# A hybrid state-space layer: C loaded as four 128-row blocks, B by 64-byte pieces, two reorderings and a PSUM bank of its own

## The chip, the cores and the metric

The kernel runs on one NeuronCore of a Trainium2 chip. The metric is the device time of one execution in microseconds (us); lower is better. Engines are named as in the profile: PE (TensorE), DVE (VectorE), ACT (ScalarE), POOL (GpSimd), SP (SyncE, which issues nearly all DMAs). All arithmetic is on float32 data.

## The reference

One decoder layer on x of 1024 positions x 1024 channels: a norm, an input projection, a state-space mixer (S5) on 512 channels, a gated short convolution on the other 512, an output projection, a residual add and a last norm.

```python
xn = rmsnorm(h, norm_gain[l])
proj = jnp.einsum('bld,dc->blc', xn, w_in[l])
...
bb_re = q_re[..., None] * b_re - q_im[..., None] * b_im
bb_im = q_re[..., None] * b_im + q_im[..., None] * b_re
bu_re = jnp.einsum('blgh,gph->blgp', u32, bb_re)
...
y = (jnp.einsum('blgp,ghp->blgh', s_re, c_re.astype(f32))
     - jnp.einsum('blgp,ghp->blgh', s_im, c_im.astype(f32))
     + d_skip.astype(f32) * u32)
...
h = h + jnp.einsum('blc,cd->bld', y, w_out[l])
return rmsnorm(h, final_norm_gain)
```

There are 32 groups g of 16 channels h, each with 64 complex states p. B is [g, p, h] and C is [g, h, p], each with a real and an imaginary part, 128 KB a part.

## The kernel before

Each matrix is split in a high part and a rest, and a product is the sum of three matmul passes: high x high ("h" in the code's tables), rest of x ("x") and rest of the weight ("l"). x is held as 8 row tiles x0 to x7 (row i of 8 consecutive positions); tiles are worked in four pairs, each of which gives 256 columns of the transposed input, a "quarter".

**The first stage** is an order written out by hand in the string `START`; inside it PE, ACT and DVE keep the order in which the code issues. Its words: `sN` squares row tile N on ACT and accumulates (L192); `nAB` is the norm of two tiles on DVE (L92 to L98 and L203); `tP` transposes pair P on PE (L211); `gP` ("gain") writes that pair's high parts `xh` from PSUM on ACT (L218); `xP` ("rest") writes the rest `xl` on DVE (L224); `uBQ...` are products of column block B with quarter Q on PE (L230), and `U` takes several blocks in turn; `kBH` copies block B's finished half H from PSUM to a tile `us` on ACT (L243) and stores it to HBM with four DMAs (L245); `dN` issues N more steps of the discretisation, a long chain of small DVE operations on [128, 32] tiles (L288); `p0`, `p1`, `p2` transpose parameters on PE (L260 to L265 and L275) and evict them on ACT; `C` copies C into another layout on ACT (L435). Products of four blocks use four PSUM banks (pool `pmm`), so a bank for quarter 2 is free only when `k` has copied that block's first half out. `us` has two buffers, so the third store copy waits for the first one's four stores, and the fourth copy for the second's.

**Parameters.** C and B are loaded with 32 rows (one group each) of 4 KB, C into `craw` (L173, L174), B into the upper 32 rows of `cb` (L176); the word `C` puts C beside it. Then `p1` and `p2` make 32 transposes of [64, 128] on PE (L275), and eight ACT instructions (L277) write b1, b2, c1 and c2 of [128, 32, 16], 128 being 64 states twice, with the signs. The discretisation multiplies b1 and b2 into bb and bs.

**DMAs** are issued by SP in program order and go to one queue on 16 DMA engines. Each DMA holds one of eight semaphores in turn, so SP doesn't issue a DMA before the one issued eight earlier has landed. A copy is cut into pieces, each a run of bytes that is contiguous on both sides.

**The middle stage** works through the string `ORDER`: projections for the convolution (tiles h, c, b, z) on PE, between them the state-space steps. `ssm_prep` makes rr (L499 to L501) and vv (L503 to L505) on DVE, rotation tables ec, and ee. `ssm_lags` multiplies bb and vv on PE (L544, `ps_k`), `ssm_in` and `ssm_out` follow (`ps_s`, `ps_y`). Its weight splits are a copy on ACT (L105) and a subtraction on DVE (L106). They share the four weight buffers with the first stage.

**The last stage** multiplies by w_out by a seven-product scheme on half matrices, for four row pairs j (L819), adds the products to the residual rows xa and xb on DVE (L823), squares them on ACT with accumulation (L826), forms 1/sqrt on DVE (`rsqrt_steps`, L92 to L98) and stores the rows. In the last pair the final product into xb's first half is made in two quarters of 256 columns in the PSUM bank `pw`, each followed by its add, its square, and a multiplication by the gain on POOL (L894). Row xa is scaled on ACT (L886) and stored (L887) before these quarters; xb's halves are scaled on DVE (L898) and ACT (L899) and stored (L901). The bank `pw` also holds the sum of three earlier products, which each quarter accumulates onto.

Of the kernel before, what the change touches and what calls it, by code (L numbers as in the profile page):

```python
# [19 lines left out]
P = 128  # L20
# [5 lines left out]
NB = 4  # L26
# [6 lines left out]
START = ("s0 w0 n0 c s1 W0 n1 W1 w1 t0 L0 g0 L1 U010hl x0 u010x. W2 s2 s3 W3 L2 n23 u20hx u30hx t1 L3 g1 u230l. s4 x1 s5 n45 "  # L33
         "U01231h u01lx. k00 p0 u11lx. k10 t2 u21lx. k20 u31lx. k30 d12 g2 s6 x2 s7 C n67 d12 U01232h u01232l t3 g3 d8 x3 u01232x. "
         "U01233h u03l p1 p2 u03x. k01 u13lx. k11 d u23lx. k21 u33lx. k31")
# [22 lines left out]
def hybrid_kernel(ctx: ExitStack, tc, x, norm_gain, w_in, a_re, a_im, log_dt, b_re, b_im,  # L58
# [70 lines left out]

    cb = big.tile([2 * NG, 3 * S * H], F32, tag="cy", name="cb")  # L130
    cb = cb.rearrange("g (r p h) -> g r p h", h=H, r=3)
    craw = pst.tile([NG, 2, H, S], F32, name="craw")
    lam_r = pst.tile([NG, 2, 2, S], F32, name="lam_r")
# [38 lines left out]
    load((4, 5, 6, 7))  # L172
    nc.sync.dma_start(craw[:, 0], c_re[0])  # L173
    nc.sync.dma_start(craw[:, 1], c_im[0])  # L174
    for k, src in enumerate((b_re, b_im, b_re)):
        nc.sync.dma_start(cb[NG:2 * NG, k], src[0])  # L176

# [73 lines left out]
    c2 = par.tile([P, NG, H], F32, name="c2")  # L251
    b1 = pst.tile([P, NG, H], F32, name="b1")
    b2 = pst.tile([P, NG, H], F32, name="b2")
    dT = par.tile([H, NG], F32, name="dT")

    def transpose_params(part):
# [13 lines left out]
        off = part - 1  # L270
        for q in range(2):
            hs = slice(q * 8, q * 8 + 8)
            ps = psm.tile([P, 8, 2 * NG], F32, tag="sm", name=f"ps_cb{off}{q}")
            for h in range(8):
                PE.transpose(ps[:, h], cb[:, off:off + 2, :, 8 * q + h].rearrange("g r p -> g (r p)"), ident[0:2 * NG, 0:2 * NG])  # L275
            for dst, lo, scale in ((b2 if off else b1, NG, nsgn if off else 1.0), (c2 if off else c1, 0, -1.0 if off else sgn)):
                A.activation(dst[:, :, hs], ps[:, :, lo:lo + NG].rearrange("p h g -> p g h"), AF.Copy, scale=scale)  # L277

# [145 lines left out]
    with tc.manual_schedule(engines={mybir.EngineType.PE, mybir.EngineType.Activation, mybir.EngineType.DVE}):  # L424
        for what in START.split():
# [5 lines left out]
            elif what[0] == "d":  # L431
                discretise(int(what[1:]) if what[1:] else None)
            elif what[0] == "C":
                for k in range(3):
                    A.copy(cb[0:NG, k], craw[:, k % 2].rearrange("g h p -> g p h"))  # L435
            elif what[0] == "c":
# [378 lines left out]
    def mult(ps, op_a, op_b, j, first, cols=slice(0, 512)):  # L815
        out_ = ps[:, 0:cols.stop - cols.start]
        for m, (p, q) in enumerate(((0, 0), (0, 1), (1, 0))):
            for k in range(NB):
                PE.matmul(out_, aq[op_a, j][:, p, k], bq[op_b, k][:, q, cols], start=first and m + k == 0,  # L819
                          stop=m == 2 and k == NB - 1, skip_group_check=True)  # L820

    def add(x, ps):
        V.tensor_tensor(x, x, ps, ADD)  # L823
# [23 lines left out]
    for j in pairs:  # L847
# [36 lines left out]
        for op in ops:  # L884
            op()
        A.activation(xa, ga, AF.Copy, scale=r)  # L886
        nc.sync.dma_start(out_ci[:, 2 * j, :], xa)  # L887
        steps, r = rsqrt_steps([part[:, 2:3], part[:, 3:4], part[:, 4:5]])
        for q in range(2):
            c = slice(q * 256, q * 256 + 256)  # L890
            mult(pw[j][:, c], "A22", "T4", j, False, c)
            add(xb[:, c], pw[j][:, c])
            final_square(xb[:, c], part[:, 3 + q:4 + q])
            Q.tensor_tensor(gb[:, c], xb[:, c], g2b[:, c], MUL)  # L894
            steps.pop(0)()
        for step_ in steps:
            step_()
# [35 lines left out]
```

## Time and profile before

| | us |
|---|---|
| runs | 432.88, 433.24, 431.73 (median 432.88) |
| the profiled execution, its time | 432.44 |
| its span (first to last record) | 430.7 |
| PE busy | 418.2 (97% of the span) |
| DVE busy | 330.1 (77%) |
| ACT busy | 182.5 (42%) |
| POOL busy | 34.6 (8%) |
| mean share of the 16 DMA engines, queue of SP | 35.6% |

A timeline row gives start, length, engine, source line, operation, output <- inputs, shape and count; in brackets stands how long the engine was idle before it and what ended that. Matmuls overlap, so a row's length is a little more than the distance to the next one. A window row gives the window, its length, each engine's busy time (and count) where engines were asked for, the granted TensorE clock as a share of full speed, the mean share of the DMA engines and GB/s. SPq is the sequencer that issues DMAs.

### The profile page before, as it was taken

What the parts mean: (1) busy time and instruction counts of PE and PEld (TensorE: products, weight loads), DVE (VectorE), ACT (ScalarE), POOL (GpSimd) and SP (SyncE); (2) the same over time, 40 slices, a digit from 0 to 9 for tenths busy, and PEclk for the clock granted to TensorE, in tenths of its full rate; (3) what the DMA queues carried; (4) which work ended last, traced back from release to release, by engine and by line L of the source; (5) the groups of instructions that cost most, each with busy time, mean ns of one, the idle gap of its engine ahead of it and who ended that gap; (6) DMA issues with size and microseconds to landing.
All of it is one profiled execution on the core that took longest, in us unless ns stands there. A gap on an engine that the chain in (4) does not pass through costs nothing.

```text
span 430.7 us, 6302 instructions
## 1 busy us (share of the span) xinstructions
PE 418.2 (97%) x2226; PEld 358.0 (83%) x2226; DVE 330.1 (77%) x820; ACT 182.5 (42%) x323; POOL 34.6 (8%) x41
## 2 busy tenths in 40 slices
PE   8998999999999999999999999999999999999992
PEld 7898999888888888888888888888888888888881
DVE  4973888869998999986996928747366799978644
ACT  5754933163313255036224415647434664333113
POOL 0000003000020020100021000211102100000022
PEclk9999989999999999999999999999999999999998
DMA  8883004523170552264025421578444450233212
GB/s 256 251 244 81 20 2 137 157 76 122 18 201 5 148 146 60 64 157 138 7 46 139 127 82 68 180 201 252 108 121 73 131 138 1 99 109 136 97 49 98
DMA packets 49471, 48.96 MB, mean 114 GB/s; under 512 B 6696, under 2 KB 39488, under 8 KB 49440
## 3 DMA queue, kind: packets, MB, share of 16 engines
q1 hardware_dynamic: 47712, 45.42, 35.6%
q0 software_dynamic: 1728, 3.15, 4.2%
q8 instruction: 17, 0.28, 0.3%
q14 instruction: 14, 0.11, 0.1%
HBM read 31.65 MB, written 8.39 MB: 93 GB/s over the span
## 4 chain that ended last, share of the span: by engine, by line
PE 95%; DMA 2%; DVE 1%; ACT 1%; issue 1%; SPq 1%; ACTq 0%
PE mm_u L230 11%; PE mm_b L230 10%; PE mm_h L230 10%; PE mm_z L230 10%; PE mm_c L230 10%; PE mm_zs L230 10%; PE ow L819 10%; PE oz L819 5%; PE glu L747 5%; PE ox L819 3%; PE ps_s L569 2%; PE ps_k L544 2%; PE ps_y L593 2%; DMA wru<-in_w_in_dram 2%; PE ps_y L594 2%; PE ps_x L211 1%
## 5 line engine op out<-in xcount | busy, mean ns | idle before, releaser
L641 POOL TENSOR_TENSOR cy<-cy,sg 128x512 f32<-128x512 f32 x8 | 13.8, 1729 | 185.5 <-DVE sg L640 152.8
L826 ACT ACTIVATE sq<-xr 128x512 f32<-128x512 f32 (+1 forms) x17 | 10.3, 605 | 38.7 <-DVE xr L823 27.2
L747 PE MATMUL glu<-shl,wg 128*128 128x512 f32 x96 | 21.9, 389 | 0.0
L747 PEld LDWEIGHTS glu<-shl,wg 128*128 128x128 f32 x96 | 18.0, 188 | 3.7
L224 DVE SCALAR_TENSOR_TENSOR xl<-ps_x,g,xh 128x256 fp32r<-128x256 f32 x32 | 12.9, 476 | 8.5 <-ACT xh L218 8.5
L230 PE MATMUL mm_u<-xh,whu 128*128 128x256 f32 x128 | 17.5, 288 | 1.7 <-ACT xh L218 1.7
L230 PE MATMUL mm_u<-xl,whu 128*128 128x256 f32 x128 | 18.3, 293 | 0.0
L230 PE MATMUL mm_u<-xh,wlu 128*128 128x256 f32 x128 | 18.3, 289 | 0.0
L230 PEld LDWEIGHTS mm_u<-xh,whu 128*128 128x128 f32 x128 | 16.2, 191 | 2.4 <-ACT xh L218 2.2
L819 PE MATMUL ow<-bs,ax 128*128 128x512 f32 (+1 forms) x54 | 16.9, 367 | 0.5 <-DVE xr L823 0.5
L230 PEld LDWEIGHTS mm_u<-xl,whu 128*128 128x128 f32 x128 | 16.9, 200 | 0.1
L230 PEld LDWEIGHTS mm_u<-xh,wlu 128*128 128x128 f32 x128 | 16.8, 197 | 0.1
L230 PE MATMUL mm_b<-xh,whb 128*128 128x512 f32 x64 | 16.6, 398 | 0.0
L230 PE MATMUL mm_h<-xh,wlh 128*128 128x512 f32 x64 | 16.2, 393 | 0.0
L230 PE MATMUL mm_h<-xh,whh 128*128 128x512 f32 x64 | 16.1, 391 | 0.0
L230 PE MATMUL mm_b<-xl,whb 128*128 128x512 f32 x64 | 15.9, 390 | 0.0
L230 PE MATMUL mm_h<-xl,whh 128*128 128x512 f32 x64 | 15.8, 389 | 0.0
L230 PE MATMUL mm_c<-xh,whc 128*128 128x512 f32 x64 | 15.8, 389 | 0.0
L230 PE MATMUL mm_z<-xh,wlz 128*128 128x512 f32 x64 | 15.8, 389 | 0.0
L230 PE MATMUL mm_c<-xl,whc 128*128 128x512 f32 x64 | 15.8, 389 | 0.0
L230 PE MATMUL mm_z<-xl,whz 128*128 128x512 f32 x64 | 15.8, 389 | 0.0
L230 PE MATMUL mm_zs<-xh,wlzs 128*128 128x512 f32 x64 | 15.8, 389 | 0.0
(354 smaller groups left out, 1108.4 us busy)
## 6 DMA issues: line engine op xcount, KB each, us to landing
ee<-ec SPq DMA_DIRECT2D x16, 256.0 KB
wro<-in_w_out_dram SPq DMA_DIRECT2D x8, 512.0 KB
xr<-in_x_dram SPq DMA_DIRECT2D x8, 512.0 KB
out_dram<-xr SPq DMA_DIRECT2D x7, 512.0 KB
x<-in_x_dram SPq DMA_DIRECT2D x6, 512.0 KB
wrh<-in_w_in_dram SPq DMA_DIRECT2D x4, 512.0 KB
wrc<-in_w_in_dram SPq DMA_DIRECT2D x4, 512.0 KB
uscr<-us SPq DMA_DIRECT2D x32, 64.0 KB
```

Source lines behind the costliest of these rows:

```text
L211: PE.transpose(pss[kt // 2][:, kt % 2, j], x_t[2 * pair + j][:, kt * P:(kt + 1) * P], ident)
L224: V.scalar_tensor_tensor(xl[pair // 2][:, kt, n], ps, g1[:, kt:kt + 1], hs.bitcast(F32), MUL, SUB)
L230: PE.matmul(ps[:, n], a[:, kt], b[half][:, kt, n], start=what == "h" and kt == 0, stop=last and kt == KT - 1)
L544: PE.matmul(ps[:, g], bb[:, g0 + 4 * q + g], vv[:, 4 * q + g, 0:T].rearrange("p t h -> p (t h)"), start=True, stop=True)
L569: PE.matmul(ps[:, g - 4 * q], w1[:, g], u2[:, g], start=True, stop=True)
L593: PE.matmul(ps[:, k], tp[:, g], u2[:, g], start=True, stop=False)
L594: PE.matmul(ps[:, k, 1:C], vv[:, g, 1:T + 1].rearrange("p t h -> p (t h)"), xa[:, g, 0:C - 1], start=False, stop=True)
L641: Q.tensor_tensor(yb[:, n], yb[:, n], sg, MUL)
L747: PE.matmul(ps, wg[:, a, k, es], shl[half][:, y, k], start=m + k == 0, stop=m == 2 and k == NB - 1)
L819: PE.matmul(out_, aq[op_a, j][:, p, k], bq[op_b, k][:, q, cols], start=first and m + k == 0, stop=m == 2 and k == NB - 1, skip_group_check ...
L826: A.activation(temp(f"sq{final_square.n}")[:, 0:x.shape[-1]], x, AF.Square, accum_out=acc)
```

## The change

Four edits stand in one diff.

1. C is loaded three times (real, imaginary, real) as four blocks of 128 rows (g, h), in pieces of 256 B. `p1` and `p2` each make four transposes of [128, 128] and one eviction. The word `C` and its copies are gone, and so is the tile `cb`.
2. B is loaded straight into the layout of b1 and b2 by four DMAs of 2,048 pieces of 64 B; b2 gets its sign from one ACT instruction behind the evictions. The tiles b1 and b2 are allocated earlier.
3. In `START`, `g2` stands ahead of `k20` and `k30`, and the high x high products of quarter 2 take blocks 0 and 1 first, then 2 and 3.
4. In the last pair, the sum held in `pw` for columns 256 to 511 is added to xb before the quarters, the second quarter's product starts anew in a bank `ol`, and row xa is scaled and stored behind the quarters.

```diff
--- before.py
+++ after.py
@@ -31,7 +31,7 @@
 EPS = 1e-6
 WARM = (26, 8, 14)
 START = ("s0 w0 n0 c s1 W0 n1 W1 w1 t0 L0 g0 L1 U010hl x0 u010x. W2 s2 s3 W3 L2 n23 u20hx u30hx t1 L3 g1 u230l. s4 x1 s5 n45 "
-         "U01231h u01lx. k00 p0 u11lx. k10 t2 u21lx. k20 u31lx. k30 d12 g2 s6 x2 s7 C n67 d12 U01232h u01232l t3 g3 d8 x3 u01232x. "
+         "U01231h u01lx. k00 p0 u11lx. k10 t2 g2 u21lx. k20 u31lx. k30 d12 s6 x2 s7 n67 d12 U012h U232h u01232l t3 g3 d8 x3 u01232x. "
          "U01233h u03l p1 p2 u03x. k01 u13lx. k11 d u23lx. k21 u33lx. k31")
 ORDER = "p0 0 1 2 m0 q0 i0 3 p1 4 5 o0 6 m1 q1 i1 7 p2 8 o1 9 m2 q2 i2 10 p3 11 o2 m3 q3 i3 12 13 o3 14 15"
 MAGIC = 12582912.0
@@ -127,9 +127,7 @@
     par = tc.alloc_tile_pool(name="par", bufs=1)
     xpool = tc.alloc_tile_pool(name="xstage", bufs=8)
 
-    cb = big.tile([2 * NG, 3 * S * H], F32, tag="cy", name="cb")
-    cb = cb.rearrange("g (r p h) -> g r p h", h=H, r=3)
-    craw = pst.tile([NG, 2, H, S], F32, name="craw")
+    craw = pst.tile([P, NB, 3, S], F32, name="craw")
     lam_r = pst.tile([NG, 2, 2, S], F32, name="lam_r")
     ldt = pst.tile([P, NG], F32, name="ldt")
     d_r = pst.tile([NG, H], F32, name="d_r")
@@ -170,10 +168,13 @@
     nc.sync.dma_start(rows, conv_w[0].rearrange("k (b p) -> (k b) p", p=P))
     nc.sync.dma_start(rowb, b_glu[0].rearrange("(b p) -> b p", p=P))
     load((4, 5, 6, 7))
-    nc.sync.dma_start(craw[:, 0], c_re[0])
-    nc.sync.dma_start(craw[:, 1], c_im[0])
-    for k, src in enumerate((b_re, b_im, b_re)):
-        nc.sync.dma_start(cb[NG:2 * NG, k], src[0])
+    for k, src in enumerate((c_re, c_im, c_re)):
+        nc.sync.dma_start(craw[:, :, k], src[0].rearrange("(b g) h p -> (g h) b p", g=G))
+    b1 = pst.tile([P, NG, H], F32, name="b1")
+    b2 = pst.tile([P, NG, H], F32, name="b2")
+    for dst, srcs in ((b1, (b_re, b_im)), (b2, (b_im, b_re))):
+        for k, src in enumerate(srcs):
+            nc.sync.dma_start(dst[k * S:k * S + S], src[0].rearrange("g p h -> p g h"))
 
 
     pw = pmm.tile([P, P], F32, tag="mm", name="ps_warm")
@@ -249,8 +250,6 @@
     lam = par.tile([P, 2, NG], F32, name="lam")
     c1 = par.tile([P, NG, H], F32, name="c1")
     c2 = par.tile([P, NG, H], F32, name="c2")
-    b1 = pst.tile([P, NG, H], F32, name="b1")
-    b2 = pst.tile([P, NG, H], F32, name="b2")
     dT = par.tile([H, NG], F32, name="dT")
 
     def transpose_params(part):
@@ -268,13 +267,13 @@
             A.copy(dT, ps[0:H, 16:16 + NG])
             return
         off = part - 1
-        for q in range(2):
-            hs = slice(q * 8, q * 8 + 8)
-            ps = psm.tile([P, 8, 2 * NG], F32, tag="sm", name=f"ps_cb{off}{q}")
-            for h in range(8):
-                PE.transpose(ps[:, h], cb[:, off:off + 2, :, 8 * q + h].rearrange("g r p -> g (r p)"), ident[0:2 * NG, 0:2 * NG])
-            for dst, lo, scale in ((b2 if off else b1, NG, nsgn if off else 1.0), (c2 if off else c1, 0, -1.0 if off else sgn)):
-                A.activation(dst[:, :, hs], ps[:, :, lo:lo + NG].rearrange("p h g -> p g h"), AF.Copy, scale=scale)
+        ps = psm.tile([P, NB, P], F32, tag="sm", name=f"ps_c{off}")
+        for b in range(NB):
+            PE.transpose(ps[:, b], craw[:, b, off:off + 2].rearrange("q r p -> q (r p)"), ident)
+        dst, scale = ((c1, sgn), (c2, -1.0))[off]
+        A.activation(dst.rearrange("p (b g) h -> p b (g h)", b=NB), ps, AF.Copy, scale=scale)
+        if off:
+            A.activation(b2, b2, AF.Copy, scale=nsgn)
 
 
 
@@ -430,9 +429,6 @@
                 warm(WARM[n[0]])
             elif what[0] == "d":
                 discretise(int(what[1:]) if what[1:] else None)
-            elif what[0] == "C":
-                for k in range(3):
-                    A.copy(cb[0:NG, k], craw[:, k % 2].rearrange("g h p -> g p h"))
             elif what[0] == "c":
                 ps = pmm.tile([P, KT], F32, tag="mm", name="ps_g1")
                 PE.transpose(ps, g1r, ident[0:KT, 0:KT])
@@ -883,16 +879,20 @@
         ops, r = rsqrt_steps([part[:, 0:1], part[:, 1:2]])
         for op in ops:
             op()
-        A.activation(xa, ga, AF.Copy, scale=r)
-        nc.sync.dma_start(out_ci[:, 2 * j, :], xa)
+        ra = r
         steps, r = rsqrt_steps([part[:, 2:3], part[:, 3:4], part[:, 4:5]])
+        pl = psm.tile([P, 512], F32, tag="sm", name="ol")
+        add(xb[:, 256:512], pw[j][:, 256:512])
         for q in range(2):
             c = slice(q * 256, q * 256 + 256)
-            mult(pw[j][:, c], "A22", "T4", j, False, c)
-            add(xb[:, c], pw[j][:, c])
+            bank = pl if q else pw[j][:, c]
+            mult(bank, "A22", "T4", j, q == 1, c)
+            add(xb[:, c], bank[:, 0:256])
             final_square(xb[:, c], part[:, 3 + q:4 + q])
             Q.tensor_tensor(gb[:, c], xb[:, c], g2b[:, c], MUL)
             steps.pop(0)()
+        A.activation(xa, ga, AF.Copy, scale=ra)
+        nc.sync.dma_start(out_ci[:, 2 * j, :], xa)
         for step_ in steps:
             step_()
         V.tensor_scalar_mul(xb[:, lo_], gb[:, lo_], r)
```

The order on ACT behind the transposes of the third pair (x4, x5). `us20` and `us30` are the third and fourth store copies, `xh1` the high parts from pair 2 (`ps_x2`) and pair 3 (`ps_x3`), `ss6` and `ss7` the squares. Before:

```order
L243 COPY us10_596<-mm_u10_306 128x512
L243 COPY us20_638<-mm_u20_400 128x512
L243 COPY us30_660<-mm_u30_417 128x512
L218 ACTIVATE xh1_85<-ps_x20_602,g1_111 128x256 x2
L218 ACTIVATE xh1_85<-ps_x21_603,g1_111 128x256 x2
L218 ACTIVATE xh1_85<-ps_x22_604,g1_111 128x256 x2
L218 ACTIVATE xh1_85<-ps_x23_605,g1_111 128x256 x2
L192 ACTIVATE ysb_83,ss6_686<-x6_118 128x1024
L192 ACTIVATE ysb_83,ss7_696<-x7_119 128x1024
L435 COPY cb_103<-craw_104 32x1024 x3
L218 ACTIVATE xh1_85<-ps_x30_805,g1_111 128x256 x2
```

Now the same stretch of ACT's order reads (source lines here are those of the changed kernel):

```order
L244 COPY us10_597<-mm_u10_307 128x512
L219 ACTIVATE xh1_85<-ps_x20_603,g1_110 128x256 x2
L219 ACTIVATE xh1_85<-ps_x21_604,g1_110 128x256 x2
L219 ACTIVATE xh1_85<-ps_x22_605,g1_110 128x256 x2
L219 ACTIVATE xh1_85<-ps_x23_606,g1_110 128x256 x2
L244 COPY us20_647<-mm_u20_401 128x512
L244 COPY us30_669<-mm_u30_418 128x512
L193 ACTIVATE ysb_83,ss6_687<-x6_117 128x1024
L193 ACTIVATE ysb_83,ss7_697<-x7_118 128x1024
L219 ACTIVATE xh1_85<-ps_x30_803,g1_110 128x256 x2
```

The four rows of high parts from `ps_x2` moved from behind the store copies of blocks 2 and 3 to ahead of them; the squares now follow the store copies directly, and the three copies of `craw` are gone.

The order on SP between the last x tile and the stores of the first two `us` tiles. Before:

```order
L148 DMA x7_119<-in_x_dram 128x1024
L173 DMA craw_104<-in_ssm_c_re_dram 32x1024
L174 DMA craw_104<-in_ssm_c_im_dram 32x1024
L176 DMA cb_103<-in_ssm_b_re_dram 32x1024
L176 DMA cb_103<-in_ssm_b_im_dram 32x1024
L176 DMA cb_103<-in_ssm_b_re_dram 32x1024
L245 DMA uscr_151<-us00_563 8x16x128 x4
L245 DMA uscr_151<-us10_596 8x16x128 x4
```

Now SP issues there:

```order
L146 DMA x7_118<-in_x_dram 128x1024
L172 DMA craw_103<-in_ssm_c_re_dram 128x4x64
L172 DMA craw_103<-in_ssm_c_im_dram 128x4x64
L172 DMA craw_103<-in_ssm_c_re_dram 128x4x64
L177 DMA b1_147<-in_ssm_b_re_dram 64x32x16
L177 DMA b1_147<-in_ssm_b_im_dram 64x32x16
L177 DMA b2_148<-in_ssm_b_im_dram 64x32x16
L177 DMA b2_148<-in_ssm_b_re_dram 64x32x16
L246 DMA uscr_154<-us00_564 8x16x128 x4
L246 DMA uscr_154<-us10_597 8x16x128 x4
```

The loads stand at the same place, five became seven, and their shapes show the pieces: [128, 4, 64] and [64, 32, 16] in place of [32, 1024].

The order on DVE in the tail, from the 1/sqrt of row xa (`vh_14`, `t_14`, `y_14`; its number 15 is row xb's) to the first step of row xb's. Before:

```order
L98 SCALAR_TENSOR_TENSOR y_14_3978<-t_14_3979,y_14_3978 128x1
L94 SCALAR_TENSOR_TENSOR vh_15_3991<-ssp3_3900,vh_15_3991 128x1
L97 SCALAR_TENSOR_TENSOR t_14_3979<-y_14_3978,vh_14_3977 128x1
L98 SCALAR_TENSOR_TENSOR y_14_3978<-t_14_3979,y_14_3978 128x1
L97 SCALAR_TENSOR_TENSOR t_14_3979<-y_14_3978,vh_14_3977 128x1
L98 SCALAR_TENSOR_TENSOR y_14_3978<-t_14_3979,y_14_3978 128x1
L823 TENSOR_TENSOR xr31_3748<-xr31_3748,ow3_3857 128x256
L94 SCALAR_TENSOR_TENSOR vh_15_3991<-ssp3_3900,vh_15_3991 128x1
L95 TENSOR_SCALAR y_15_3992<-vh_15_3991 128x1
L97 SCALAR_TENSOR_TENSOR t_15_3993<-y_15_3992,vh_15_3991 128x1
```

Now DVE's order there is:

```order
L98 SCALAR_TENSOR_TENSOR y_14_3945<-t_14_3946,y_14_3945 128x1
L94 SCALAR_TENSOR_TENSOR vh_15_3956<-ssp3_3867,vh_15_3956 128x1
L97 SCALAR_TENSOR_TENSOR t_14_3946<-y_14_3945,vh_14_3944 128x1
L98 SCALAR_TENSOR_TENSOR y_14_3945<-t_14_3946,y_14_3945 128x1
L819 TENSOR_TENSOR xr31_3715<-xr31_3715,ol_3959 128x256
L97 SCALAR_TENSOR_TENSOR t_14_3946<-y_14_3945,vh_14_3944 128x1
L98 SCALAR_TENSOR_TENSOR y_14_3945<-t_14_3946,y_14_3945 128x1
L94 SCALAR_TENSOR_TENSOR vh_15_3956<-ssp3_3867,vh_15_3956 128x1
L95 TENSOR_SCALAR y_15_3957<-vh_15_3956 128x1
```

The add of the second quarter (now from `ol`) stands two operations earlier, inside the 1/sqrt of row xa.

## The prediction

> **What bounds the kernel now.** I read the page's busy table first, then PE's waits, then the timeline of each engine around the places that the change touches, and last the DMA shares there.
>
> ```profile
> span 430.7 us, 6302 instructions
> PE 418.2 (97%) x2226; PEld 358.0 (83%) x2226; DVE 330.1 (77%) x820; ACT 182.5 (42%) x323; POOL 34.6 (8%) x41
> ```
> ```profile
> PE mm_u L230 <- ACT xh L218: 1.7, 2, 1.1
> ```
>
> TensorE (PE) works 418.2 of 430.7 us, and between the start and the tail its one wait of size is the 1.1 us on `xh`. So only three things can pay here: PE's own work, that wait, and the tail after PE's last product. Everything else is cover, and the question is how thin the cover is. PE's timeline between 38 and 105 us shows the places (start, length, operation, count, idle before):
>
> ```profile
> 38.77 1.12 PE L230 MATMUL mm_u<-xl,whu 128*128 128x256 f32 x8
> 40.98 4.10 PE L230 MATMUL mm_u<-xh,whu 128*128 128x256 f32 x32 [1.10 <-ACT xh L218]
> 48.76 1.91 PE L211 MATMUL ps_x<-ident,x 128*128 128x128 f32 x16
> 50.43 4.08 PE L230 MATMUL mm_u<-xl,whu 128*128 128x256 f32 x32
> ...
> 59.23 3.79 PE L275 MATMUL ps_cb<-ident,cb 64*128 64x64 f32 x32
> 62.95 2.07 PE L230 MATMUL mm_u<-xl,whu 128*128 128x256 f32 x8
> 64.82 1.54 PE L230 MATMUL mm_u<-xh,wlu 128*128 128x256 f32 x8
> 66.19 1.12 PE L230 MATMUL mm_u<-xl,whu 128*128 128x256 f32 x8
> ...
> 104.63 1.27 PE L544 MATMUL ps_k<-vv,bb 128*16 128x128 f32 x10
> ```
>
> Right behind the 32 parameter transposes PE runs at half its granted clock; the windows say so (length, PE busy, clock, DMA share, GB/s):
>
> ```profile
> 62.95:64.82 1.87, 1.87 (x9) 0.50 0.00 0
> 66.19:67.16 0.97, 0.97 (x11) 1.00 0.00 0
> ```
>
> **The change, part by part: PE.** (a) With the third pair's high parts ahead of the two store copies on ScalarE (ACT), `xh` is ready before PE wants it: 1.10 us. (b) The 32 transposes hold PE from 59.23 to 62.95, 3.72 us. Eight of 128x128 take their place; 16 of that form went from 48.76 to 50.43, 1.67 us, so eight cost 0.84. Saved: 2.88. (c) The eight products after them took 1.87, the next eight 1.37, where eight at full clock take 0.97: 1.30 lost to the clock. I count that as gone, since the 16 larger transposes at 48.76 were followed by no slow products. PE's own gain is 5.3 us.
>
> **VectorE (DVE) lets less through.** ACT's and DVE's timelines, same columns:
>
> ```profile
> 34.35 0.59 ACT L243 COPY us<-mm_u 128x512 f32<-128x512 f32 x1 [1.61 <-PE mm_u L230]
> ...
> 39.97 0.59 ACT L243 COPY us<-mm_u 128x512 f32<-128x512 f32 x1 [1.33 <-PE mm_u L230]
> 40.45 3.04 ACT L218 ACTIVATE xh<-ps_x,g 128x256 fp32r<-128x256 f32 x8
> 43.32 1.12 ACT L192 ACTIVATE ysb<-x 128x1024 f32<-128x1024 f32 x1
> ...
> 45.52 0.18 ACT L192 ACTIVATION_READ_ACCUMULATOR ysb<-x 128x1 f32 x1
> 45.61 5.94 ACT L435 COPY cb<-craw 32x1024 f32<-32x1024 f32 x3
> 51.46 2.96 ACT L218 ACTIVATE xh<-ps_x,g 128x256 fp32r<-128x256 f32 x8
> ```
> ```profile
> 45.74 0.15 DVE L92 TENSOR_SCALAR vh<-ss 128x1 f32<-128x1 f32 x1 [1.03 <-ACT ysb L192]
> ...
> 52.54 3.22 DVE L224 SCALAR_TENSOR_TENSOR xl<-ps_x,g,xh 128x256 fp32r<-128x256 f32 x8
> ...
> 66.14 1.23 DVE L106 TENSOR_TENSOR wlh<-wrh,whh 128x1024 fp32r<-128x1024 f32 x1 [0.83 <-ACT whh L105]
> ...
> 102.98 1.35 DVE L505 TENSOR_TENSOR vv<-vv,tv 128x1152 f32<-128x1152 f32 x1
> ```
>
> `vv` is finished at 104.33, and PE reads it at 104.63: 0.30 us of slack. So PE arrives at `ps_k` no more than 0.3 us earlier than DVE does, plus what DVE itself gains. DVE's long scalar chain starts behind the norm at 45.74, which waits for the squares of x6 and x7, finished at 45.70. Those now follow the store copies directly: the second copy still waits for PE and runs 39.97 to 40.56, the squares take 43.32 to 45.70, 2.38 us, so they end at 42.94 and the norm starts 2.8 us earlier. From there DVE runs on; its 0.83 us wait at 66.14 is for a weight buffer that PE frees, and PE is there 5.3 us earlier, so it goes too. DVE gains 3.6 us, PE at `ps_k` 3.6 + 0.3 = 3.9. The other 1.4 us of PE's gain become a new wait at `ps_k`. Behind it everything moves together.
>
> At no cost: the `C` copies that go (5.94 us) only delayed the last `xh` to 51.46, and DVE's row at 52.54 had no idle before it; of PE's 1.7 us of waits on `xh`, 1.10 are those at 40.98 and the rest is at the start. The two new copies from PSUM and the scaling of `b2` are 128x512 like the store copy's 0.59 us, 1.8 us in place of eight evictions; but the scaling stands in ACT's queue ahead of the weight copies, and if the B loads were not there by about 59 us all those would stall. The rest x2 on DVE now runs in DVE's idle time before 41.
>
> **The loads: the unknown price.** C was two loads of 32 rows of 4 KB; it is now three of 512 pieces of 256 B (1,536). B was three of 32 rows; it is now four of 2,048 pieces of 64 B (8,192). They queue behind the x loads, and the stores of `us` queue behind them (all 32 stores, then DMA windows: length, clock, DMA share, GB/s):
>
> ```profile
> L245 SPq DMA_DIRECT2D uscr<-us x32: 570/575/716, 32.5 to 96.9; - x32
> ```
> ```profile
> 24.00:28.00 4.00, 1.00 1.04 339
> 28.00:32.00 4.00, 1.00 0.63 129
> 119.00:119.60 0.60, 1.00 1.09 322
> 129.95:130.20 0.25, 1.00 0.32 33
> 425.00:426.00 1.00, 1.00 0.94 389
> ```
>
> Where the queue reaches C: C and B were 0.655 MB, of which 129 GB/s x 4 us = 0.52 MB went after 28.0, the other 0.14 MB at 339 GB/s before it, so from 27.6 us. For 64-byte pieces the nearest row is 129.95: the last `tp` copy, 128 pieces, 8 KB, alone. Its engines were 32% busy, 16 x 0.25 x 0.32 / 128 = 10 ns a piece; at that, B takes 8,192 x 10 / 16 = 5.1 us. The other end: 128 pieces in the whole 0.25 us gives 16 us. Between lies the pace of 512-byte pieces (119.00: 322 GB/s / 512 B = 629 a us): 13.0 us. I take 6.5, near the low end, because that lone copy had only eight pieces per engine and its engines stood two thirds idle, which a queue of 512 per engine will not. C: 1.2 us by bytes, 2.4 by pieces, I take 2.2. So B ends at 27.6 + 2.2 + 6.5 = 36.3.
>
> What that meets: `us` has two buffers, and SP has at most eight loads or stores open, so the fourth store of the second `us` waits until the last B load has landed. I estimate 4.0 us from B's last piece to that store's landing (landing 1.3, issue 0.6, the store 2.1; now the second copy ends at 34.94, its four stores are issued by 37.2 at 0.575 us each, and they were done by 39.97, so a store lands within 2.8 us of its issue). Then the fourth store copy starts at 36.3 + 4.0 = 40.3 instead of 39.97: 0.3 us late, and with it squares, norm and DVE's chain. The head gives 3.9 - 0.3 = 3.6. From here each us of B's time costs one.
>
> The Trainium skill speaks against this ("DMA: Bandwidth & Descriptors", section Why small descriptors are slow (HBM only)): a fixed overhead of about 3 cycles a packet weighs on small pieces from HBM, and copies within SBUF are spared. My row is such a copy, so no run here shows the price from HBM; taking 64 B as 2 cycles, 2 + 3 make 2.5 times the price, an estimate by that page of 12.8 us for B instead of 5.1, and a sum of 434.2 us instead of 427.9.
>
> **The tail.** PE, DVE, ACT:
>
> ```profile
> 420.93 0.51 PE L819 MATMUL ow<-bs,ax 128*128 128x256 f32 x2 [0.51 <-DVE xr L823]
> ```
> ```profile
> 420.46 0.42 DVE L823 TENSOR_TENSOR xr<-xr,ow 128x256 f32<-128x256 f32 x1 [0.74 <-PE ow L819]
> ...
> 422.47 0.22 DVE L97 SCALAR_TENSOR_TENSOR t<-y,vh 128x1 f32<-128x1 f32 x1
> ...
> 422.80 0.42 DVE L823 TENSOR_TENSOR xr<-xr,ow 128x256 f32<-128x256 f32 x1
> 424.63 0.16 DVE L94 SCALAR_TENSOR_TENSOR vh<-ssp,vh 128x1 f32<-128x1 f32 x1 [1.42 <-ACT sq L826]
> ```
> ```profile
> 420.97 0.42 ACT L826 ACTIVATE sq<-xr 128x256 f32<-128x256 f32 x1 [0.44 <-DVE xr L823]
> ...
> 423.05 1.15 ACT L886 ACTIVATE xr<-ysb,y 128x1024 f32<-128x1024 f32 x1 [1.57 <-DVE y L98]
> 424.11 0.40 ACT L826 ACTIVATE sq<-xr 128x256 f32<-128x256 f32 x1
> ...
> 426.36 0.72 ACT L899 ACTIVATE xr<-ysb,y 128x512 f32<-128x512 f32 x1 [1.76 <-DVE y L98]
> ```
>
> The own bank spares PE 0.51 us, but the last add was not waiting for PE alone: it stood behind two small DVE operations from 422.47. It now stands ahead of them, 422.45 instead of 422.80. The last square followed its add by 0.51 us in the first quarter (420.46 to 420.97), here by 1.31, since ACT was in the 1.15 us copy of row xa. With that copy behind it the square starts at 422.96 instead of 424.11: 1.15 us earlier, and the chain behind it with it. The xa copy then fills ACT's 1.76 us gap. Its store is issued some 0.6 us later than now while the last two come 1.15 earlier; 512 KB at 389 GB/s are 1.35 us, so they may meet: I take 0.25 off. Tail: 0.9 us.
>
> **Sum.** 3.6 + 0.9 = 4.5 us, from the profiled execution's own 432.44 (span 430.7): 427.9 us. The median of the runs shown, 432.88, is 0.44 above it, within their 431.73 to 433.24.
>
> **Rivals.** (1) *64-byte pieces at the 512-byte pace or slower.* Place: the ring ahead of the `us` stores; the fourth store copy is late, its PSUM bank blocks PE, its squares DVE. At 13.0 us B ends 42.8, 6.5 later than forecast: 434.4 us; at 16 us 437.4. It decides from the point where 4.5 us are lost, B over 11.0 us. For it: the one 64-byte row is neither from HBM nor long. Against: 10 ns of engine time there. The Trainium skill's section named above would put it here. (2) *A middling price, 8 to 11 us*: 429.4 to 432.4. (3) *DVE does not hold PE back*, because the slack at `ps_k` refills otherwise: all 5.3 and 1.15 us come, 432.44 - 6.45 = 426.0. Against: `vv`'s end at 104.33. (4) *The head is hidden anyway*, DVE's chain not moving (something on ACT or a load ahead of `vv` that I don't see): the tail and 0.3 us, 431.2. Against: DVE's rows at 52.54 and 102.98 have no idle before them.
>
> **Chances.** Forecast 0.45 (its own range 427 to 429), (1) 0.18, (2) 0.20, (3) 0.09, (4) 0.08. Against 432.88, 0.3% is 1.3 us, about what a measurement of this kernel tells from no change: faster below 431.6, slower above 434.2. Faster: 0.45 + 0.09 + 0.16 of (2) + 0.04 of (4) = 0.74; slower: 0.12 of (1); same: 0.14. The range reaches from (3), 426.0, to 433.5, B at some 12 us; it leaves out about 0.05 below and 0.15 above.
>
> **What would show it.** In the profile after: no wait on `xh` at 40 us, transposes of 0.84 us, clock 1.00 behind them, the norm of x6 and x7 at 43 to 43.3 us, a new wait of PE at `ps_k` of 1 to 1.7 us, the last square directly behind its add. I am wrong if the fourth store copy starts after 41 us on a DMA, if PE stands before the products of blocks 2 and 3, or if PE doesn't wait for `vv`.

## The result, and the profile after

Four runs of the changed kernel lie between 428.69 and 429.13 us, median 429.01; beside them four of the kernel before have a median of 433.03. The ratio is 0.9912, 95% interval 0.9892 to 0.9933: faster by 4.0 us. The profiled execution took 428.69 us, 3.75 less than the profiled one before, where 4.5 were forecast. Three executions behind the table of experiments were in a slow state (527.76, 1,480.0 and 1,557.41 us): its ratios leave them out, its medians do not (without its slow one, experiment 8 has a median of 427.23).

The page of the changed kernel, span and busy times, and the end of its table of PE's waits (total, count, longest):

```profile
span 426.8 us, 6246 instructions
PE 414.9 (97%) x2202; PEld 354.7 (83%) x2202; DVE 331.2 (78%) x821; ACT 175.6 (41%) x315; POOL 34.6 (8%) x41
```
```profile
PE ps_k L540 <- DVE vv L501: 0.8, 1, 0.8
PE mm_c L231 <- DVE vp L614: 0.7, 1, 0.7
PE mm_b L231 <- ACT us L244: 0.6, 1, 0.6
PE mm_u L231 <- ACT xh L219: 0.4, 1, 0.4
```

PE works 3.3 us less, and three waits are new. PE's timeline shows what goes and what comes (start, length, operation, count, idle before):

```profile
39.33 4.24 PE L231 MATMUL mm_u<-xh,whu 128*128 128x256 f32 x32
...
57.63 1.04 PE L272 MATMUL ps_c<-ident,craw 128*128 128x128 f32 x8
58.42 1.19 PE L231 MATMUL mm_u<-xl,whu 128*128 128x256 f32 x8
59.45 1.12 PE L231 MATMUL mm_u<-xh,wlu 128*128 128x256 f32 x8
...
82.43 2.11 PE L231 MATMUL mm_c<-xh,whc 128*128 128x512 f32 x8 [0.72 <-DVE vp L614]
...
88.73 2.12 PE L231 MATMUL mm_b<-xh,whb 128*128 128x512 f32 x8 [0.55 <-ACT us L244]
...
101.58 1.26 PE L540 MATMUL ps_k<-vv,bb 128*16 128x128 f32 x10 [0.78 <-DVE vv L501]
```

The wait on `xh` at 40 us is gone (the 0.4 left is at the start), the transposes take 0.79 us to the next row instead of 3.72, and the eight products behind them take 1.03 instead of 1.87. So PE was 5.8 us ahead of before at 65 us, 0.4 of it from an earlier start. At `ps_k` it is 3.05 ahead (104.63 to 101.58): 2.05 went into the three new waits, and the other 0.7 lies around them (PE's last products run out before a wait begins, and the first behind two of them are slower, 2.11 instead of 1.98). From there to the tail the distance stays.

ACT's timeline shows where the head fell short, in the third and fourth store copies (L244):

```profile
35.04 3.03 ACT L219 ACTIVATE xh<-ps_x,g 128x256 fp32r<-128x256 f32 x8 [0.51 <-PE ps_x L212]
38.61 0.58 ACT L244 COPY us<-mm_u 128x512 f32<-128x512 f32 x1 [0.55 <-DMA uscr<-us]
40.88 0.58 ACT L244 COPY us<-mm_u 128x512 f32<-128x512 f32 x1 [1.68 <-DMA uscr<-us]
41.36 1.06 ACT L193 ACTIVATE ysb<-x 128x1024 f32<-128x1024 f32 x1
```

Both wait for stores on DMA queues; before, both waited for PE. SP's timeline says why: SP issues in order, and was busy or held with B until 33.27 us, so the first store, ready at 32.03, was issued at 33.37.

```profile
24.56 0.74 SPq L177 DMA_DIRECT2D b<-in_ssm_b_re_dram  x1
25.34 6.66 SPq L177 DMA_DIRECT2D b<-in_ssm_b_im_dram  x2
32.05 1.22 SPq L177 DMA_DIRECT2D b<-in_ssm_b_re_dram  x1
33.37 1.28 SPq L246 DMA_DIRECT2D uscr<-us  x1
```

The norm of x6 and x7 starts at 43.73 us, 2.0 earlier than before, where 2.5 were forecast (2.8 less the 0.3 of the late store copy). In the tail, ACT's timeline has the last square 0.51 us behind its add (419.29), and row xa's copy behind it:

```profile
419.80 0.42 ACT L822 ACTIVATE sq<-xr 128x256 f32<-128x256 f32 x1 [1.39 <-DVE xr L819]
...
420.69 1.15 ACT L894 ACTIVATE xr<-ysb,y 128x1024 f32<-128x1024 f32 x1 [0.39 <-DVE vh L94]
```

### The profile page after: what moved, and what is told of

It is laid out like the page before. It is cut to its first block, busy times and chain, and to the rows that moved or that the text cites. A ratio compares the mean times of both kernels' runs of the same rounds, so it can differ in the third digit from the quotient of the medians.

```text
span 426.8 us, 6246 instructions
## 1 busy us (share of the span) xinstructions
PE 414.9 (97%) x2202; PEld 354.7 (83%) x2202; DVE 331.2 (78%) x821; ACT 175.6 (41%) x315; POOL 34.6 (8%) x41
## 4 chain that ended last, share of the span: by engine, by line
PE 83%; DVE 11%; ACT 2%; DMA 2%; issue 1%; SPq 1%; ACTq 0%; DVEq 0%
PE mm_zs L231 10%; PE ow L815 10%; PE mm_b L231 9%; PE mm_z L231 9%; PE mm_h L231 8%; PE mm_c L231 8%; PE mm_u L231 7%; PE glu L743 5%; PE oz L815 5%; PE ox L815 3%; DVE e L287 2%; PE ps_s L565 2%; PE ps_k L540 2%; PE ps_y L589 2%; PE ps_y L590 2%; DMA wru<-in_w_in_dram 2%
## 5 line engine op out<-in xcount | busy, mean ns | idle before, releaser
L219 ACT ACTIVATE xh<-ps_x,g 128x256 fp32r<-128x256 f32 x32 | 12.1, 486 | 9.6 <-PE ps_x L212 9.6
L231 PE MATMUL mm_b<-xh,wlb 128*128 128x512 f32 x64 | 15.8, 389 | 0.0
L231 PE MATMUL mm_c<-xh,wlc 128*128 128x512 f32 x64 | 15.8, 389 | 0.0
L231 PE MATMUL mm_zs<-xh,whzs 128*128 128x512 f32 x64 | 15.8, 389 | 0.0
```

The lines of the kernel that those rows point to most:

```text
L219: A.activation(xh[pair // 2][:, kt, n], ps, AF.Copy, scale=g1[:, kt:kt + 1])
L231: PE.matmul(ps[:, n], a[:, kt], b[half][:, kt, n], start=what == "h" and kt == 0, stop=last and kt == KT - 1)
```

## The experiments

Each series of four kernels was timed on one chip beside the kernel before.

| | median us | before, same series | ratio | 95% interval |
|---|---|---|---|---|
| 1 changed, tail of before | 429.76 | 432.61 | 0.9927 | 0.9907 to 0.9948 |
| 2 changed, row xa written ahead | 429.50 | 432.61 | 0.9930 | 0.9903 to 0.9956 |
| 3 before, new order alone | 431.54 | 432.61 | 0.9981 | 0.9965 to 0.9996 |
| 4 before, new loads alone | 430.23 | 432.61 | 0.9948 | 0.9928 to 0.9968 |
| 5 changed, other DVE form | 428.57 | 432.75 | 0.9902 | 0.9884 to 0.9919 |
| 6 changed, B late | 428.07 | 432.75 | 0.9894 | 0.9877 to 0.9911 |
| 7 changed, B twice | 434.85 | 432.75 | 1.0052 | 1.0032 to 1.0071 |
| 8 = 5 and 6 | 427.61 | 432.75 | 0.9869 | 0.9850 to 0.9888 |
| 9 changed, again | 429.00 | 432.86 | 0.9920 | 0.9892 to 0.9949 |
| 10 = 8, again | 427.61 | 432.86 | 0.9884 | 0.9856 to 0.9913 |
| 11 before, other DVE form | 433.24 | 432.86 | 1.0008 | 0.9990 to 1.0027 |
| 12 changed, ACT's order by hand | 429.22 | 432.86 | 0.9924 | 0.9898 to 0.9950 |

My theory was the prediction's: DVE's chain from the norm of x6 and x7 to `vv` holds PE at `ps_k`, B's loads set that norm, and in the tail ACT's order pays. The rivals: PE's own savings arrive whatever DVE does, the loads are covered, the bank pays.

**1 and 2, the tail.** Experiment 1 puts the tail of before into the changed kernel. Experiment 2 keeps the bank and moves two lines back:

```diff
-        ra = r
+        A.activation(xa, ga, AF.Copy, scale=r)
+        nc.sync.dma_start(out_ci[:, 2 * j, :], xa)
...
-        A.activation(xa, ga, AF.Copy, scale=ra)
-        nc.sync.dma_start(out_ci[:, 2 * j, :], xa)
```

> The changed kernel with the tail of before (row xa scaled and stored ahead of the quarters, both quarters in one bank). My theory: the tail's edit is worth 0.8 us, all of it behind PE's last product, so 429.0 + 0.8 = 429.8 us; PE's rows up to the last product as in the changed kernel, and the last square again 1.3 us behind its add. Rival (the tail gives nothing of its own, and the whole difference of 4.0 us is made in the first stage): 429.0 us.

> The changed kernel, but with row xa's scaling and store back ahead of the two quarters; the own bank and the early add stay. My theory: the tail's gain comes from ACT's order alone, so the last square stands behind the 1.15 us copy of row xa again and at most 0.35 of the 1.15 us is kept: 429.5 to 429.8 us. Rival (the bank that spares PE's 0.51 us wait is what pays): 429.0 us, as the changed kernel.

The time of so small a step drowns in the intervals; the traces don't. From the start of `ps_k` to the end of the span, experiment 1 takes 427.0 - 101.17 = 325.8 us, the changed kernel 426.8 - 101.58 = 325.2. Experiment 2 takes 427.1 - 101.96 = 325.1, all of the gain, and ACT's timeline there shows the reason:

```profile
420.14 0.42 ACT L822 ACTIVATE sq<-xr 128x256 f32<-128x256 f32 x1 [1.38 <-DVE xr L819]
...
421.04 1.15 ACT L882 ACTIVATE xr<-ysb,y 128x1024 f32<-128x1024 f32 x1 [0.39 <-DVE vh L94]
```

Row xa's copy (L882) stands behind the last square though the code has it ahead: the scheduler puts it there once the bank and the early add are in. So this run did not separate order from bank, and my expectation failed. Experiment 12 fixes ACT's order by hand, with one bank and no early add:

```diff
+        with tc.manual_schedule(engines={mybir.EngineType.Activation}):
+            for q in range(2):
...
+                mult(pw[j][:, c], "A22", "T4", j, False, c)
+                add(xb[:, c], pw[j][:, c])
...
+            A.activation(xa, ga, AF.Copy, scale=ra)
```

> The changed kernel with both quarters in one bank and no early add, as in the tail of before, but with ACT's order fixed by hand: both last squares first, then row xa's copy. My theory: of the 1.11 us by which the last stores come earlier in the changed kernel, ACT's order gives 0.8 and the bank with the early add 0.35; so the last square follows its add by 0.5 us, the last store is issued 321.5 us behind ps_k (322.28 with the tail of before, 321.17 in the changed kernel), and the time is 429.3 us. Rival (the bank gives it all): 322.3 us behind ps_k, 429.8 us.

Its ACT and SP timelines:

```profile
420.87 0.42 ACT L822 ACTIVATE sq<-xr 128x256 f32<-128x256 f32 x1 [1.82 <-DVE xr L819]
...
421.28 1.13 ACT L892 ACTIVATE xr<-ysb,y 128x1024 f32<-128x1024 f32 x1
```
```profile
422.44 0.33 SPq L893 DMA_DIRECT2D out_dram<-xr  x1
423.75 0.83 SPq L899 DMA_DIRECT2D out_dram<-xr  x2
```

The last pair of stores is issued 423.75 - 102.22 = 321.53 us behind `ps_k`, as expected, against 423.45 - 101.17 = 322.28 in experiment 1 and 422.75 - 101.58 = 321.17 in the changed kernel: order 0.75, bank and add 0.36. In the span the bank's share does not show: span minus `ps_k` is 325.2 here too. In the changed kernel the last stores follow row xa's more closely (0.88 us instead of 1.31), which may be why; no run shows it.

**3 and 4, order and loads apart.** Experiment 3 has only `START`'s new order (with `C` behind s7), experiment 4 only the loads and transposes (without `C`).

> The kernel before with the first stage's new order alone (third pair's high parts ahead of two store copies, products of quarter 2 by pairs of blocks); loads, copies of C, 32 small transposes and tail stay as they were. My theory: DVE's norm of x6 and x7 comes at 43.0 instead of 45.7 us, but PE only loses its wait of 1.1 us on xh, arrives at ps_k 1.1 us earlier and doesn't wait for vv, which is 2.7 us earlier: 431.9 us. The half clock behind the 32 transposes stays. Rival (DVE's chain from the norm alone sets the head): 2.7 us, 430.3 us.

> The kernel before with the new loads of C and B and the 8 large transposes alone (no copies of C); order and tail as before. My theory: the store copies of blocks 2 and 3 wait for stores that stand behind B in SP's order (38.6 and 40.9 us), the third pair's high parts and the squares stand behind them, so the norm of x6 and x7 is 1 us later than before (46.7); PE's 2.88 + 1.30 us of saved work turn into a wait of 3 us or more at ps_k, and the time is 433.0 to 433.7 us. Rival (PE's own savings arrive at the end whatever DVE does): 433.0 - 4.2 + 0.9 = 429.7 us.

Experiment 3 gives 0.8 us, near the 1.1 of the wait on `xh`, and PE does not wait for `vv`, which ends at 101.87 us, 2.4 ahead of `ps_k`. DVE's chain alone sets nothing there. Experiment 4 gives 2.25 us, where I expected none. Its fourth store copy starts at 41.21 on a DMA and the norm at 46.97, 1.2 later than before, as expected; but PE passes `ps_k` at 102.34 with a wait of 0.67. My rule that `vv` keeps its distance from the norm failed: 55.3 us here, 58.6 before. DVE's waits for weight copies are gone (0.83 and 0.92 before), and on ACT `whh` stands ahead of `rotc`, so that `whc` follows `rotc` by 3.44 us instead of 4.40. The rest is a row that I had taken for plain work. DVE's timeline in the changed kernel:

```profile
69.49 1.95 DVE L287 TENSOR_SCALAR e<-ap 128x32 f32<-128x32 f32 x1
```

and GpSimd's (POOL):

```profile
69.56 1.85 POOL L484 MEMSET tp<- 128x1024 f32 x2
```

DVE's and GpSimd's in experiment 4:

```profile
75.20 0.33 DVE L287 TENSOR_SCALAR e<-ap 128x32 f32<-128x32 f32 x1
```
```profile
73.65 1.84 POOL L484 MEMSET tp<- 128x1024 f32 x2
```

In both, the small instruction ends 0.03 or 0.04 us after the memsets do (71.41 and 75.49). In experiment 4 it arrived when they were nearly over. DVE's timeline in the kernel before has the long row too, but there a subtraction (`wlb`) ran beside it, so that less was lost:

```profile
72.54 1.96 DVE L288 TENSOR_SCALAR e<-ap 128x32 f32<-128x32 f32 x1
72.92 1.57 DVE L106 TENSOR_TENSOR wlb<-wrb,whb 128x1024 fp32r<-128x1024 f32 x1
```

**5 and 11, the same row in another form**, in the changed kernel and in the one before:

```diff
-    step(V.tensor_scalar, pre, ap[:, 0, :, 1], 1.0, None, SUB)
+    step(V.tensor_tensor, pre, ap[:, 0, :, 1], ap[:, 0, :, 0], SUB)
```

> The changed kernel with one DVE instruction in another form: real part of a minus 1 as a subtraction of the tile's column of ones (tensor_tensor) instead of a tensor_scalar with the constant 1. In the changed kernel that tensor_scalar takes 1.95 us, from 69.49 to 71.44, and GpSimd's two memsets run from 69.56 to 71.41 us. My theory: DVE's chain from the norm of x6 and x7 over rot, ACT's whc and vv sets when PE passes ps_k, and this instruction stands in it; in the new form it takes 0.2 us, vv ends 1.6 us earlier, PE's waits on vv, vp and the us copies (0.78, 0.72, 0.55) shrink by as much: 429.0 - 1.6 = 427.4 us. Rival 1 (the memset blocks DVE whatever the instruction's form): 429.0, the next row is long instead. Rival 2 (the chain is covered, PE is held by something else): the row is short, but the time stays 429.0.

> The kernel before with the subtraction in the other form alone. There PE never waits for vv (vv ends at 104.33, PE reads it at 104.63 us), so by my theory the instruction gets short (0.2 us instead of 1.96), but no time is won: 432.8 us, within 0.3 us. Rival (DVE's time counts as such, before as after): 1.1 us faster, 431.7 us.

DVE's and GpSimd's timelines in experiment 5:

```profile
69.73 0.20 DVE L287 TENSOR_TENSOR e<-ap 128x32 f32<-128x32 f32 x1
...
70.07 1.22 DVE L106 TENSOR_TENSOR wlb<-wrb,whb 128x1024 fp32r<-128x1024 f32 x1
...
72.20 1.23 DVE L106 TENSOR_TENSOR wlz<-wrz,whz 128x1024 fp32r<-128x1024 f32 x1 [0.32 <-ACT whz L105]
```
```profile
69.80 1.84 POOL L484 MEMSET tp<- 128x1024 f32 x2
```

The row is short beside the same memsets, so the form decides, and rival 1 falls. `vv` ends 56.5 us behind the norm instead of 57.8; PE's waits on `vp` and the us copies are gone, that on `vv` is 0.39. Of 1.6 us 1.3 come, 0.3 being a new wait on `whz`. The gain over the changed kernel, 0.4 to 0.8 us by the ratios, lies within the intervals. In the kernel before the same edit brings `vv` 1.0 us forward (103.34 instead of 104.33) and, by the medians, no time, as expected. Its trace is of the fastest of its executions (431.31 us), in which PE did not lose time to the clock behind the transposes and read `vv` at 103.40, 0.06 us after its end; there the edit may have paid.

**6, 7 and 9, the price of B.** Experiment 6 issues B's loads behind the fourth store copy's stores, experiment 7 loads B twice, experiment 9 changes nothing.

```diff
+    def load_b(us):
+        for dst in (b1, b2):
+            Q.tensor_copy(dst[:, 0, 0:1], us[:, 3, C - 1:C])
...
+                nc.sync.dma_start(dst[k * S:k * S + S], src[0].rearrange("g p h -> p g h"))
```

> The changed kernel with B's four loads issued behind the fourth store copy's stores instead of ahead of the first ones (two one-column writes on GpSimd hold them back; nothing else moves on any engine). My theory: SP is held by issuing B until 33.4 us and B's pieces delay the stores, so the third and fourth store copies (38.61 and 40.88 in the changed kernel, 0.55 and 1.68 us of waits on DMA) come 0.5 and 1.2 to 1.7 us earlier, the norm of x6 and x7 and vv 1.2 to 1.7 us: 427.3 to 427.8 us. Rival 1 (store copies wait for PE, not for the loads): 429.0. Rival 2 (B now comes too late for p2's scaling of b2 on ACT at 59 us, which stands ahead of the weight copies): slower than 429.5.

> The changed kernel with B loaded a second time right behind the first, into tiles that nothing reads: 8,192 more pieces of 64 B ahead of the stores of us. My theory: each us by which B's loads end later costs one, since the fourth store copy, the squares, the norm and the products of blocks 2 and 3 stand behind them; B took 8.9 us from 27.0 to 35.9 us, so 8 to 8.9 us more: 437.0 to 438.0 us. Rival (PE's lead of 5.8 us at 65 us, most of it lost at later waits, takes up to 2 us of it): 435 to 436. Rival (loads are covered): 429.0.

> The changed kernel once more, nothing edited, beside the two candidates of this series and with a second trace. 429.0 us. In its first trace PE's first products began at 11.66 us, in the traces of the experiments at 12.4 to 13.1 us. My theory: the store copies of blocks 2 and 3 waited 0.55 and 1.68 us for DMAs there because that start was early; with a start 1 us later PE itself is what they wait for, and the fourth one starts at 40.5 to 41.3 us all the same. Rival: they wait as long whatever the start, and the norm of x6 and x7 comes 1 us later than 43.73 us.

Read from the traces, in us; "copy" is the fourth store copy's start, "after" its distance from PE's first product:

| trace | first product | first us store | copy | after | waits for | norm | vv ends | vv - norm |
|---|---|---|---|---|---|---|---|---|
| before | 12.05 | 32.47 | 39.97 | 27.92 | PE | 45.74 | 104.33 | 58.6 |
| changed | 11.66 | 33.37 | 40.88 | 29.22 | DMA | 43.73 | 101.52 | 57.8 |
| 9 (changed) | 12.52 | 34.00 | 41.37 | 28.85 | DMA | 44.22 | 102.04 | 57.8 |
| 12 | 12.19 | 34.31 | 41.50 | 29.31 | DMA | 44.35 | 102.16 | 57.8 |
| 2 | 12.47 | 33.26 | 41.27 | 28.80 | DMA | 44.12 | 101.91 | 57.8 |
| 5 | 13.10 | 33.72 | 41.10 | 28.00 | DMA | 43.95 | 100.44 | 56.5 |
| 1 | 12.57 | 32.98 | 40.48 | 27.91 | PE | 43.33 | 101.11 | 57.8 |
| 6, B late | 12.87 | 33.29 | 40.79 | 27.92 | PE | 43.64 | 101.49 | 57.9 |
| 10, B late | 12.63 | 33.05 | 40.55 | 27.92 | PE | 43.40 | 100.55 | 57.2 |

PE alone lets the copy start 27.9 us after its first product. With B ahead of the stores it starts 0 to 1.4 us later than that, with B behind them in neither trace. Experiment 9's expectation failed: with PE's start 0.9 us later the copy still waited 1.85 us for a DMA. What goes with the lateness is how far SP's first `us` store lies behind PE's start: 21.7, 21.5, 22.1 and 20.8 us in the four late traces, 20.4 in experiments 1, 6 and 10, 20.6 in experiment 5. The norm follows the copy by 2.85 us in every row but the first. In time, experiment 6 is 0.8 to 1.1 us ahead of the changed kernel by the ratios, less than the 1.2 to 1.7 expected and with overlapping intervals; its one trace lost 0.8 us behind `ps_k`, 0.5 of it at a wait that the others don't have (`mm_zs` for `sgl`).

Experiment 7 prices the pieces. SP's timeline, PE's waits, PE's timeline and a window row of PE:

```profile
33.18 1.42 SPq L182 DMA_DIRECT2D b<-in_ssm_b_re_dram  x1
34.64 2.80 SPq L182 DMA_DIRECT2D b<-in_ssm_b_im_dram  x2
37.48 1.46 SPq L182 DMA_DIRECT2D b<-in_ssm_b_re_dram  x1
39.04 10.62 SPq L251 DMA_DIRECT2D uscr<-us  x16
```
```profile
PE mm_u L236 <- ACT us L249: 4.3, 2, 2.6
```
```profile
44.74 0.58 PE L236 MATMUL mm_u<-xh,whu 128*128 128x256 f32 x1 [2.61 <-ACT us L249]
47.02 1.22 PE L236 MATMUL mm_u<-xh,whu 128*128 128x256 f32 x4 [1.71 <-ACT us L249]
...
106.24 1.26 PE L545 MATMUL ps_k<-vv,bb 128*16 128x128 f32 x10
```
```profile
48.00:50.00 2.00, 2.00 (x12) 0.50 0.40 104
```

The stores come 39.04 - 33.37 = 5.7 us later, the fourth copy 46.39 - 40.88 = 5.5, the end 5.85 (434.85 against 429.0), below the 437 to 438 that I expected and just below the rival's 435 to 436. So a us of B costs about one, but not on the path that I had named. PE doesn't wait for `vv` here (it ends at 105.83, and `ps_k` starts at 106.24 with no idle before it). PE itself stood 4.3 us before the products of blocks 2 and 3, and then lost some 2 us more to the clock, which was at half from 44.5 to 51.3 us; against that, its three waits of the changed kernel are gone. That the sum comes near 5.5 is partly chance.

8,192 pieces more cost 5.5 us and not 8 to 8.9: the first 8.9 also held C's pieces and time in which the DMA engines had little to do (18% busy from 32 to 33 us). 5.5 us x 16 engines / 8,192 = 10.7 ns a piece, if the engines are busy throughout (their share was 0.89 to 1.23 from 34 to 42 us). My estimate of 12.8 us, worked out from the Trainium skill ("DMA: Bandwidth & Descriptors", Why small descriptors are slow (HBM only)), is not borne out: a piece from HBM costs about the 10 ns of the copy within SBUF.

**8 and 10, both edits.** Experiment 10 is the kernel of experiment 8 again, for a trace.

> The edits of the two runs above together, the subtraction in the other form and B's loads late. My theory: DVE's chain is 2.8 to 3.3 us earlier, more than the 2.05 us that PE waits for it in the changed kernel (0.78, 0.72, 0.55), so PE's own work is the bound and only 2.0 us come: 427.0 us, with no wait of PE on vv. Rival (the two gains add up, as PE's lead of 5.8 us in the first stage is fully kept): 429.0 - 2.8 = 426.2 us. Rival (no chain of DVE holds PE): 429.0.

> The kernel with the subtraction in the other form and B's loads late, unedited, for its trace. My theory: 427.5 us; PE waits at ps_k for vv 0.4 us or less, and neither for vp nor for the us copies. Against the changed kernel in the same series: 1.1 to 1.6 us faster. Rival (the gain of its first timing was chance): within 0.5 us of the changed kernel.

Experiment 8 took 427.61 us where I expected 427.0. In the series that has both the changed kernel and this one, the changed kernel ran 428.31 to 430.46 us and this one 427.19 to 428.11, medians 1.4 apart as expected. It is the fastest kernel of this study, 0.9884 of the one before (0.9856 to 0.9913). A row of PE's and one of DVE's timeline:

```profile
100.60 1.26 PE L546 MATMUL ps_k<-vv,bb 128*16 128x128 f32 x10 [0.79 <-DVE vv L507]
```
```profile
72.30 1.23 DVE L106 TENSOR_TENSOR wlz<-wrz,whz 128x1024 fp32r<-128x1024 f32 x1 [0.95 <-ACT whz L105]
```

The waits on `vp` and the us copies are gone, the one on `vv` is not: I expected 0.4 us or less. DVE now waits 0.95 us for a weight copy that comes hardly earlier than in the changed kernel (71.21 against 71.51). What that copy waits for is open; in experiment 5's trace the same copy (71.12) waits for its load `wrz`, so the load is the likely one.

## Why the prediction was right, and where its steps were off

**PE's own 5.3 us: right.** The wait, the transposes (0.79 for 0.84) and the clock came as said. But (c) is not a constant. Behind the 32 small transposes experiment 3 ran at half clock too, for 3.4 us as in the profile before (2 us windows), experiment 11 not at all. A window behind the transposes in experiment 3 (length, PE busy, clock, DMA share, GB/s):

```profile
63.60:65.00 1.40, 1.40 (x8) 0.50 0.00 0
```

and in experiment 11:

```profile
62.90:64.80 1.90, 1.90 (x17) 1.00 0.00 0
```

The executions of the kernel before point the same way: of the 50 beside the experiments, 23 have a mean clock of 0.992 or less and take 433.3 us in the mean, 21 have 0.995 or more and take 432.1. This fits a loss of 1.3 us in about half of the executions; where their clock fell is not on record.

**"From there DVE runs on": wrong, though the limit at `ps_k` was real.** The chain leaves DVE twice. ACT's timeline of the changed kernel:

```profile
85.28 0.60 ACT L287 ACTIVATE rotc<-rot 64x112 f32<-64x112 f32 x2 [12.24 <-DVE rot L287]
85.91 1.05 ACT L105 CAST whh<-wrh 128x1024 fp32r<-128x1024 f32 x1
86.86 1.21 ACT L287 ACTIVATE rotc<-rot 64x112 f32<-64x112 f32 x4
88.10 1.07 ACT L244 COPY us<-mm_u 128x512 f32<-128x512 f32 x2
89.06 0.61 ACT L612 COPY hs<-mm_h 128x512 f32<-128x512 f32 x1
89.69 1.05 ACT L105 CAST whc<-wrc 128x1024 fp32r<-128x1024 f32 x1
```

ACT stands 12 us for `rot`, the last of DVE's small steps, and behind it queue a weight copy, the us copies that free PE's banks, and `whc`, for which DVE waits. Before, the two rows were:

```profile
88.09 0.92 ACT L288 ACTIVATE rotc<-rot 64x112 f32<-64x112 f32 x3 [10.84 <-DVE rot L288]
...
92.49 1.05 ACT L105 CAST whc<-wrc 128x1024 fp32r<-128x1024 f32 x1
```

From `rotc` to `whc` it is 4.4 us, from `whc` to the end of `vv` 11.84 before (104.33) and 11.83 after (101.52). So all three new waits of PE hang on one DVE chain, and its gain, 88.09 - 85.28 = 2.81, with 0.24 of slack used up, is PE's lead at `ps_k`. The forecast was 3.6: 2.8 from the norm, 0.83 for a wait that goes, 0.3 of slack, less 0.3 for the late store copy. Measured: 2.0 from the norm and 0.8 behind it. That the 0.8 looks like the 0.83 of the forecast is luck. It is two waits gone (0.83 and 0.92, of which I had counted one) less what I did not see: the memsets' hold on DVE, beside which the subtraction `wlb` ran before, now stands bare. Some of the 2.0 is chance as well: in the other late traces of the table with B ahead (9, 12 and 2) the norm starts at 44.12 to 44.35, 1.4 to 1.6 us earlier than before.

**The fourth store copy 0.3 us late: the term that was mis-sized.** It was 0.9 to 1.4 us, counted from PE's first product, in four of six traces with these loads and this order, 0 and 0.1 in experiments 1 and 5. B's end was near the forecast (its last piece at 35.9 for 36.3), and so were the 10 ns a piece; but from that end to the copy it took 5.0 us (to 40.88) where I had 4.0, since I left out that SP, issuing in order, was not free for the first stores. By the prediction's own sign, a start after 41 us on a DMA, this step is at its edge: 40.88 in the profile after, 41.27 to 41.50 in the traces of 9, 12 and 2.

**A new wait of 1.4 us at `ps_k`:** the 2.05 us came as three waits. **The tail, 0.9:** 326.1 to 325.2 us from `ps_k` on; the split between order and add was right (0.75 and 0.36 us at the last store's issue), but with the bank and the early add in place the scheduler makes the order even without the moved line.

The parts, each alone, give 0.8 (order), 2.25 (loads) and 0.6 us (tail by its trace), 3.7 of the 4.0. Rival (3) is refuted by PE's waits on `vv`, `vp` and the us copies, (4) by DVE's chain, whose last small step comes 2.81 us earlier, (1) and (2) by B's end at 35.9 us and its price in experiment 7.

## What to carry to other kernels

When the busiest engine is sped up, follow each chain that it will meet next through every engine's queue, not along one: here the limit ran from DVE over ACT back to DVE, and an instruction queued there by chance was part of it. A short instruction that is long in the trace is a stall with a cause of its own; it can be free in one kernel and cost a microsecond in the next. A load is paid for at the issuing queue too: ask which stores stand behind it. And when a run gives the forecast number, read its waits before taking it for the forecast path: in experiment 7 the number came by another.

## What the hardware showed that was not expected

A DVE `TENSOR_SCALAR` of 128x32 took 1.95 us while GpSimd's memsets ran and ended with them, within 0.05 us, in every trace in which they met; a `TENSOR_TENSOR` of the same size (0.20 us) and one of 128x1024 (1.22 us) ran beside the memsets unhindered in experiment 5. That fits what the Trainium skill says ("SBUF — State Buffer", Who interferes with whom): DVE in its two-port modes and GpSimd exclude each other for a whole instruction. No trace shows the mode in which the `TENSOR_SCALAR` ran, and here it was held through both memsets.

8,192 pieces of 64 B from HBM took 5.5 us more, 10.7 ns of engine time each, near the 10 ns of such pieces within SBUF.

32 transposes of [64, 128] were followed by half clock in the traces of the kernel before and of experiment 3 and by full clock in that of experiment 11, with the same transposes and products; 8 of 128x128 were followed by full clock in all ten traces that have them. In experiment 7 two waits of PE, 2.61 and 1.71 us with one product between them, went over into half clock for 6.8 us; the single wait of 1.10 us in the kernel before did not.
